# Up product of a conv-gated MLP: two groups of three tiles with two seven-product tiles each, and the first down sums behind tile 4

## The chip, the cores and the metric

One core of one Trainium2 chip. TensorE (PE) multiplies; VectorE (DVE) and ScalarE (ACT) work on vectors in SBUF and PSUM; GpSimd (POOL) works in SBUF; SyncE (SP) issues DMAs. Each engine takes its instructions in the order of its own queue, and engines wait for one another by semaphores. The metric is the device time of one execution in microseconds (us), the median of several runs.

## The reference

One layer of an encoder: a retention branch and a spatial-gating branch are merged and added to x, then comes a gated MLP with a depthwise convolution of width 3. Sequence 512, model width 1024, MLP width 2816, float32. The change touches only the MLP:

```python
def _conv_gated_mlp(h, w_up, conv_w, conv_b, w_down):
    hid = h @ w_up                      # (512, 1024) @ (1024, 5632)
    hid = lax.conv_general_dilated(hid, conv_w..., padding=((1, 1),), feature_group_count=c) + conv_b
    a, b = jnp.split(hid, 2, axis=-1)
    return (jax.nn.gelu(a) * b) @ w_down
```

Every float32 product is made of three matmuls in PE's float32r format, over a high part and a low part of each operand: high x high, high x low, low x high.

## The kernel before

The stages follow each other: projections with retention, the gates, the output product and norms, then the up product of the MLP and the down product.

**Up product.** The 5632 columns make 22 tiles (`NF`) of two blocks of 128 columns, one for each half of the gate. A block computed whole is 8 depth steps x 3 matmuls of 512 columns: `up_block`, through `mm3` (lines 231 to 233). Tiles 0 and 1 are early blocks, computed in two halves among the norms; tiles 2, 3, 20 and 21 are whole. Tiles 4 to 19 come in couples: the first of a couple as seven products, the second whole.

**Seven products.** A `Pair` treats the two blocks of a tile, the two halves of the depth and the two halves of the 512 positions as a 2 x 2 block product, and makes it in Winograd's way: seven products of 4 depth steps x 3 matmuls of 256 columns (line 691) in place of eight. The weights enter in seven forms: B11, B21, T1, T2, T3, T4, B22, where the T's are sums of raw weights; the activations' sums S1 to S4 were made once. `part1` does the products with B11, B21, T1 and T2; `part2` the one with T3 and takes T4 and B22; `part3` those two. A tile's three PSUM banks are summed into two temporaries c0 and c1 by ACT copies (line 85) and DVE sums (lines 708, 719, 731). The bank of the first product (B11) is written again by the fourth (T2), so that product must wait for the copy of c0 that reads the bank.

In a couple, PE's order is: `part1`; the first block of the whole tile; `part2`; half the second block; `part3`; the other half.

**Weights.** `units` lists what is loaded and in which order; `w_get` hands out the next and issues others ahead, as far as nine slots of the pool `w4` go (a form takes one slot, a block two). For each unit SP issues the load into one of four `raw` buffers; ACT copies it into the high part (wf, wh; line 85), DVE subtracts for the low part (wf, wl; line 92). For the T forms, DVE adds raw weights for T1 and T3 (lines 170, 171) and POOL for T2 and T4 (lines 172, 174): T2 = T1 + B22, T4 = T2 + B21, the latter written over T2's raw buffer once T2 is split.

**Behind a tile.** `tile_done` runs the convolution (`conv`: one ACT row and two DVE taps, lines 1000 and 1004, for each block), the GELU on ACT (line 1011) and the gate's product on DVE (line 1013). Then, after some tiles, `down_forms` makes the sums of the down product from two finished tiles: eight DVE rows (fa, fs, fl, gp; lines 92, 1030 to 1033) and four ACT copies. The first such sums, of tiles 0 and 1, stand behind tile 7.

The order in each engine's queue is set when the program is built; nothing is reordered on the chip between rows of DVE, ACT, POOL or SP.

Of the kernel before, what the change touches and what calls it, by code (L numbers as in the profile page):

```python
# [38 lines left out]
ENDS = (0, 2, 3, 1)  # L39
UP0 = DOWN0 - 2 * NF  # L40
EARLY = 4
COUPLES = [(i, i + 1) for i in range(4, 20, 2)]

PRE, LNG, LNB = 0, 8, 16
CW, CB = 24, 24 + 3 * 2 * NF
# [5 lines left out]
def tile_block(ctx: ExitStack, tc, xT, x, wall, par, cs, wsp, bsp, gpost, gpre, gffn, out):  # L51
# [11 lines left out]
    def blk(dt=F32, n="blk", shape=(P, S)):  # L63
        return sb.tile(list(shape), dt, tag="blk", bufs=NBLK, name=nm(n))
# [4 lines left out]
    def tmp(n="tmp", shape=(P, S)):  # L69
        return sb.tile(list(shape), F32, tag="tmp", bufs=6, name=nm(n))  # L70
# [7 lines left out]
    def ps(shape=(P, S)):  # L78
        return pp.tile(list(shape), F32, tag="ps", name=nm("ps"))
# [18 lines left out]
    FORMS = ("B11", "B21", "T1", "T2", "T3", "T4", "B22")  # L98
    units = []
    i = 0  # L100
    while i < NW:
        pair = [(f, i) for f in FORMS]
        if U0 <= i < GATE0:
            units += pair
            i += 2
        elif GATE0 <= i < GATE1:
            units += pair[:4] + [("blk", i + 2)] + pair[4:] + [("blk", i + 3)]
            i += 4
        elif i == UP0 + 2 * COUPLES[0][0]:
            for a, b in COUPLES:  # L110
                pair = [(f, UP0 + 2 * a) for f in FORMS]
                units += pair[:4] + [("blk", UP0 + 2 * b)] + pair[4:] + [("blk", UP0 + 2 * b + 1)]
            i = UP0 + 2 * COUPLES[-1][1] + 2
        elif i == DOWN0:
            for _ in range(2):
                pairs = [[("q", i + j), ("t", i + j)] for j in range(DP)]
                whole = [[("blk", i + DP)], [("blk", i + DP + 1)]]
                for u in pairs[:4] + whole[:1] + pairs[4:6] + whole[1:] + pairs[6:] if i == DOWN0 else pairs + whole:
                    units += u
                i += DP + WHOLE // 2  # L120
        else:
            units.append(("blk", i))
            i += 1
# [90 lines left out]
    def w_next():  # L214
        u = units[w_pos[1]]
        w_ready[w_pos[1]] = w_unit(u)
        w_pos[1] += 1
        return w_size(u)

    def w_get(look=LOOK, most=99):  # L220

        i = w_pos[0]
        w_pos[0] += 1
        room = 2 * look + (2 if w_size(units[i]) == 2 else 0)
        n = sum(w_size(u) for u in units[i : w_pos[1]])
        while w_pos[1] < len(units) and (w_pos[1] <= i or n + w_size(units[w_pos[1]]) <= min(most, max(room, 9 if look == LOOK else 0))):
            n += w_next()
        return w_ready.pop(i)

    def mm3(o, ah, al, bh, bl, start, stop):  # L230
        nc.tensor.matmul(o, ah, bh, start=start, stop=False)  # L231
        nc.tensor.matmul(o, ah, bl, start=False, stop=False)  # L232
        nc.tensor.matmul(o, al, bh, start=False, stop=stop)  # L233
# [48 lines left out]
    for k in range(KD):  # L282
# [18 lines left out]
        for m in range(8):  # L301
            c = slice(m * P, (m + 1) * P)
# [78 lines left out]
    for m in range(8):  # L381
        t = blk(n="qkraw")
# [266 lines left out]
    for n, acc in enumerate(t_group()):  # L649
        if n == 0:  # L650
            g_turn(0)
        if n < 2:
            for k in (n + 2, n + 6):
                t = tmp("xT")
# [92 lines left out]
    uT, late = [], None  # L747
    for j in range(KD // 2):
        p = Pair(AF.Gelu_apprx_tanh, lambda: blk(n="u"), scale=rbc)
# [7 lines left out]
        late = p  # L757
# [46 lines left out]
    for j in range(KD // 2):  # L804
        for o, t in gated_pair(ogh, ogl, late if j == 0 else None):
            b = blk(n="r")
# [117 lines left out]
    def h2(k, t):  # L924
        return tuple(h[k // 2][:, k % 2, t] for h in (h2h, h2l))

    h2forms = {n: [None] * 4 for n in ("S1", "S2", "S3", "S4")}
# [8 lines left out]
    def h2_sums(i):  # L936

        a0, b0, a1, b1 = h2r[0][i], h2r[0][i + 2], h2r[1][i], h2r[1][i + 2]
        v.tensor_sub(b1, a1, b1)
        v.tensor_sub(a1, a0, a1)  # L940
        v.tensor_sub(a0, b1, a0)
        v.tensor_add(b0, b0, a0)
        for n, t in zip(("S1", "S2", "S3", "S4"), (b1, a0, a1, b0)):
            h2_parts(n, i, t)
# [9 lines left out]
    def up_block(between=None):  # L954
        (wh, wl), o = w_get(), ps()
        for k in range(KD):
            if between and k == KD // 2:
                between()
            c = slice(k * P, (k + 1) * P)
            mm3(o, wh[:, c], wl[:, c], *h2(k, slice(0, S)), k == 0, k == KD - 1)  # L960
        return o
# [33 lines left out]
    def conv(o, m):  # L995
        c = tmp("cv")
        nc.scalar.activation(
            out=c, in_=o, func=AF.Identity, scale=col(CW + 3 * m + 1), bias=col(CB + m)
        )
        v.scalar_tensor_tensor(  # L1000
            out=c[:, 1:S], in0=o[:, 0 : S - 1], scalar=col(CW + 3 * m), in1=c[:, 1:S],
            op0=ALU.mult, op1=ALU.add,
        )
        v.scalar_tensor_tensor(
            out=c[:, 0 : S - 1], in0=o[:, 1:S], scalar=col(CW + 3 * m + 2), in1=c[:, 0 : S - 1],
            op0=ALU.mult, op1=ALU.add,
        )
        return c

    def gated(ca, cb):  # L1010
        nc.scalar.activation(out=ca, in_=ca, func=AF.Gelu_apprx_tanh)
        gp.append(blk(n="gp"))
        v.tensor_mul(gp[-1], ca, cb)
# [10 lines left out]
    def down_forms(j):  # L1024

        a, b = gp[2 * j], gp[2 * j + 1]
        first = blk(F32R, "fa")
        split(first[:, T0], first[:, T1], a[:, T0])
        s_ = blk(n="fs")
        v.tensor_sub(s_[:, T0], a[:, T1], b[:, T1])  # L1030
        v.tensor_sub(s_[:, T1], s_[:, T0], a[:, T0])
        v.tensor_sub(a[:, T0], a[:, T0], a[:, T1])
        v.tensor_add(a[:, T1], b[:, T0], s_[:, T1])
        bh, bl = two_parts(b, j >= WIDE)
        sh, sl = two_parts(s_, j >= WIDE)
        th, tl = two_parts(a, j >= WIDE)
        dforms.append({
            "A11": (first[:, T0], first[:, T1]), "A12": (bh[:, T0], bl[:, T0]), "A22": (bh[:, T1], bl[:, T1]),
            "S1": (sh[:, T0], sl[:, T0]), "S2": (sh[:, T1], sl[:, T1]),
            "S3": (th[:, T0], tl[:, T0]), "S4": (th[:, T1], tl[:, T1]),  # L1040
        })

    def tile_done(i, o):
        gated(*(conv(t, 2 * i + s_) for s_, t in enumerate(o)))
        if i < COUPLES[-1][1]:
            if i in (7, 11, 13, 17):
                down_forms(len(dforms))
        elif len(dforms) < EAGER:
            down_forms(len(dforms))

    couples = dict(COUPLES)
    i = 0
    while i < NF:
        if i in couples:
            p = Pair(None, lambda: tmp("c"), h2, h2forms)
            p.part1()
            o = [up_block()]
            p.part2()
            o.append(up_block(p.part3))
            tile_done(i, p.t)  # L1060
            tile_done(i + 1, o)
            i += 2
        else:
            o = []
            for e in (2 * i, 2 * i + 1):
                o.append(early_o[e] if e < EARLY else up_block())
            if i < 2:
                h2_sums(i)
                w_next()
            tile_done(i, o)  # L1070
            i += 1
# [154 lines left out]
    for t in ENDS:  # L1226
# [10 lines left out]
        for i, (b, e) in enumerate((((M2, e1), (M3, xx)), ((M4, uu), (M8, yy)))[t // 2]):  # L1237
            f, h = slice((t % 2) * 256, (t % 2 + 1) * 256), slice(i * 256, (i + 1) * 256)
# [51 lines left out]

def _up(a):

    for i, _ in COUPLES:
        b, c = a[2 * i].reshape(P, 2, S), a[2 * i + 1].reshape(P, 2, S)
        a[2 * i : 2 * i + 2] = np.stack([
            np.concatenate([b[:, 0], c[:, 0]], -1), np.concatenate([c[:, 1], b[:, 1]], -1),
        ])
    return a
# [85 lines left out]
```

## Time and profile before

| | |
|---|---|
| median of 3 runs | 818.98 us (818.52 to 819.2) |
| the profiled execution | 818.99 us |
| its span, first to last instruction | 817.2 us |
| mean granted clock of TensorE | 0.999 |
| busy: DVE, ACT, POOL | 657.0, 430.0, 102.5 us |
| instructions | 13212 |
| loads of raw weights on SP's queue | 145, 512 KB each, 3.5 us to landing |

The page of the profile has the busy time of each engine; its matmuls are pipelined, so that a busy PE alone says little, and the chain of work that ended last and the list of waits are read beside it. A timeline row has its start, its length, the engine, the line, the operation, what it writes and reads with buffer numbers left out, the shape, and in brackets the idle time before it. Rows overlap by some 0.1 us at their ends, so that the price of a row in a busy queue is the distance to the next start.

### The profile page before, as it was taken

The numbers are of one execution on the slowest core, as the hardware profiler recorded it, in microseconds if no ns is written. First come the engines' busy times: TensorE is split into PE (matmuls) and PEld (weight loads), VectorE is DVE, ScalarE is ACT, GpSimd is POOL, SyncE is SP. The second block draws the span as 40 slices with busy tenths as digits, with TensorE's granted clock in tenths as the row PEclk, the third lists the DMA queues.
The fourth block names the chain that finished last, engine by engine and source line by source line (L and its number), as shares of the span: only waits on it lengthen the run. The fifth ranks groups of instructions, "written<-read, shape, count | busy, mean of one in ns | idle before, by whom it ended". The sixth has DMA issues, their size and how long they took to land.

```text
span 817.2 us, 13212 instructions
## 1 busy us (share of the span) xinstructions
PE 810.2 (99%) x5154; PEld 730.9 (89%) x5154; DVE 657.0 (80%) x1076; ACT 430.0 (53%) x733; POOL 102.5 (13%) x108
## 2 busy tenths in 40 slices
PE   9999999999999999999999999999999999999997
PEld 7888888888899999999988898899999998999996
DVE  7579897877898877767766579778989989898976
ACT  6636445536665544444435466455656665645532
POOL 0100000012222011132211210210201200000001
PEclk9999999999999999999999999999999999999999
DMA  8733221222234332323359212333333341234354
GB/s 284 262 117 103 77 79 65 68 75 79 91 101 133 104 93 88 103 86 103 102 175 360 87 49 73 104 103 103 104 104 103 103 140 67 78 103 129 104 181 104
DMA packets 29391, 93.76 MB, mean 115 GB/s; under 512 B 3408, under 2 KB 4304, under 8 KB 29328
## 3 DMA queue, kind: packets, MB, share of 16 engines
q1 hardware_dynamic: 26928, 86.59, 32.1%
q0 software_dynamic: 1968, 6.03, 2.4%
q8 instruction: 40, 0.66, 0.4%
q10 hardware_dynamic: 432, 0.30, 0.1%
q14 instruction: 23, 0.19, 0.1%
HBM read 88.19 MB, written 4.72 MB: 114 GB/s over the span
## 4 chain that ended last, share of the span: by engine, by line
PE 98%; DMA 0%; DVE 0%; issue 0%; ACT 0%; DVEq 0%
PE ps L691 23%; PE ps L232 13%; PE ps L231 13%; PE ps L233 13%; PE ps L1088 11%; PE ps L495 5%; PE ps L496 5%; PE ps L497 5%; PE ps L1119 2%; PE ps L846 2%; PE ps L845 2%; PE ps L847 2%; PE ps L770 1%; PE ps L295 1%; PE ps L912 0%; PE ps L620 0%
## 5 line engine op out<-in xcount | busy, mean ns | idle before, releaser
L92 DVE TENSOR_TENSOR wl<-raw,wh 128x1024 fp32r<-128x1024 f32 (+1 forms) x93 | 108.9, 1180 | 48.2 <-PE ps L691 24.2
L85 ACT ACTIVATE wf<-raw 128x512 fp32r<-128x512 f32 x140 | 84.9, 626 | 98.7 <-PE ps L232 40.2
L92 DVE TENSOR_TENSOR wf<-raw,wf 128x512 fp32r<-128x512 f32 x140 | 110.0, 802 | 26.4 <-ACT wf L85 25.6
L691 PE MATMUL ps<-sh,wf 128*128 128x256 f32 x640 | 118.8, 277 | 0.0
L85 ACT ACTIVATE wh<-raw 128x1024 fp32r<-128x1024 f32 (+2 forms) x95 | 93.0, 989 | 34.5 <-DMA raw<-wall 16.5
L691 PEld LDWEIGHTS ps<-sh,wf 128*128 128x128 f32 x640 | 100.7, 188 | 0.9 <-ACT wf L85 0.2
L231 PE MATMUL ps<-h2h,wh 128*128 128x512 f32 (+1 forms) x256 | 93.2, 364 | 0.0
L232 PE MATMUL ps<-h2l,wh 128*128 128x512 f32 (+1 forms) x256 | 93.1, 364 | 0.0
L233 PE MATMUL ps<-h2h,wl 128*128 128x512 f32 (+1 forms) x256 | 92.8, 362 | 0.0
L691 PE MATMUL ps<-sl,wf 128*128 128x256 f32 x320 | 88.5, 277 | 0.0
L495 PE MATMUL ps<-wh,xh 128*128 128x512 f32 x192 | 75.1, 391 | 0.0
L496 PE MATMUL ps<-wl,xh 128*128 128x512 f32 x192 | 74.9, 390 | 0.0
L497 PE MATMUL ps<-wh,xl 128*128 128x512 f32 x192 | 74.8, 390 | 0.0
L172 POOL TENSOR_TENSOR raw<-raw,raw 128x512 f32<-128x512 f32 x20 | 33.9, 1693 | 239.5 <-DVE raw L170 185.9
L691 PEld LDWEIGHTS ps<-sl,wf 128*128 128x128 f32 x320 | 60.1, 188 | 0.8 <-issue 0.2
L233 PEld LDWEIGHTS ps<-h2h,wl 128*128 128x128 f32 x256 | 48.3, 189 | 7.7
L231 PEld LDWEIGHTS ps<-h2h,wh 128*128 128x128 f32 x256 | 48.2, 188 | 6.9
L232 PEld LDWEIGHTS ps<-h2l,wh 128*128 128x128 f32 x256 | 48.1, 188 | 6.5
L691 PE MATMUL ps<-xh,wf 128*128 128x256 f32 x288 | 53.4, 278 | 0.0
L1088 PE MATMUL ps<-dl,fh 128*128 128x256 f32 x168 | 46.5, 277 | 0.0
L1088 PE MATMUL ps<-dh,fl 128*128 128x256 f32 x168 | 46.5, 277 | 0.0
L1088 PE MATMUL ps<-dh,fh 128*128 128x256 f32 x168 | 46.5, 277 | 0.0
(326 smaller groups left out, 2057.9 us busy)
## 6 DMA issues: line engine op xcount, KB each, us to landing
raw<-wall SPq DMA_DIRECT2D x145, 512.0 KB, 3.5
x<-x SPq DMA_DIRECT2D x20, 256.0 KB, 5.5
xT<-xT SPq DMA_DIRECT2D x8, 256.0 KB, 5.5
x<-x POOLq DMA_DIRECT2D x8, 256.0 KB, 2.6
xT<-xT POOLq DMA_DIRECT2D x4, 256.0 KB, 3.9
cs<-cs SPq DMA_DIRECT2D x2, 256.0 KB, 4.2
gpm<-gpost POOLq DMA_DIRECT2D x2, 256.0 KB, 3.9
gpr<-gpre POOLq DMA_DIRECT2D x2, 256.0 KB, 5.0
```

What stands on the lines that cost most here:

```text
L85: nc.scalar.activation(out=o, in_=i, func=AF.Copy)
L92: return nc.vector.tensor_sub(lo, src, as32(hi))
L172: nc.gpsimd.tensor_tensor(out=w_raw["T2"], in0=w_raw["T1"], in1=w_raw["B22"], op=ALU.add)
L231: nc.tensor.matmul(o, ah, bh, start=start, stop=False)
L232: nc.tensor.matmul(o, ah, bl, start=False, stop=False)
L233: nc.tensor.matmul(o, al, bh, start=False, stop=stop)
L495: nc.tensor.matmul(acc[t], xh[k][:, c], wh[:, f], start=k == 0, stop=False)
L496: nc.tensor.matmul(acc[t], xh[k][:, c], wl[:, f], start=False, stop=False)
L497: nc.tensor.matmul(acc[t], xl[k][:, c], wh[:, f], start=False, stop=k == KD - 1)
L691: nc.tensor.matmul(o, w_[:, c], a_, start=first and k == n == 0, stop=k == 3 and n == 2, skip_group_check=True,)
L845: nc.tensor.matmul(o, ah, bh, start=k == 0, stop=False)
L1088: nc.tensor.matmul(o, a_[:, c], w_[:, f], start=j == t == i == 0, stop=j == DP - 1 and i == 2 and n not in (M2, M3, M4), skip_group_check= ...
```

## The change

Tiles 4 to 9 are no longer three couples but two groups of three, (4, 5, 6) and (7, 8, 9): in each the first two tiles are made as seven products, the third whole. Nine tiles instead of eight are made as seven products. In such a group, PE's order is: `part1` of the first tile; the first block of the whole tile; `part2` of the first tile; `part1` of the second; `part3` of the first; `part2` of the second; half the second block; `part3` of the second; the other half. The unit list follows: four forms, a block, ten forms, a block. `tile_done` of the first tile is called right after its `part3`. The first `down_forms` (tiles 0 and 1) moves from behind tile 7 to behind tile 4; those behind 11, 13 and 17 stay. On the host, the raw weights of each tile are laid out for the seven products or whole, as the new list wants. From tile 10 on the couples are as before.

```diff
-COUPLES = [(i, i + 1) for i in range(4, 20, 2)]
+GROUPS = [(4, 5, 6), (7, 8, 9)] + [(i, i + 1) for i in range(10, 20, 2)]
+SUMS_AT = (4, 11, 13, 17)
...
-        elif i == UP0 + 2 * COUPLES[0][0]:
-            for a, b in COUPLES:
-                pair = [(f, UP0 + 2 * a) for f in FORMS]
-                units += pair[:4] + [("blk", UP0 + 2 * b)] + pair[4:] + [("blk", UP0 + 2 * b + 1)]
-            i = UP0 + 2 * COUPLES[-1][1] + 2
+        elif i == UP0 + 2 * GROUPS[0][0]:
+            for *a, b in GROUPS:
+                group = [(f, UP0 + 2 * t) for t in a for f in FORMS]
+                units += group[:4] + [("blk", UP0 + 2 * b)] + group[4:] + [("blk", UP0 + 2 * b + 1)]
+            i = UP0 + 2 * GROUPS[-1][-1] + 2
...
-        if i < COUPLES[-1][1]:
-            if i in (7, 11, 13, 17):
+        if i < GROUPS[-1][-1]:
+            if i in SUMS_AT:
                 down_forms(len(dforms))
...
-    couples = dict(COUPLES)
+    groups = {g[0]: g for g in GROUPS}
...
-        if i in couples:
+        if i in groups:
             p = Pair(None, lambda: tmp("c"), h2, h2forms)
             p.part1()
             o = [up_block()]
             p.part2()
+            if len(groups[i]) > 2:
+                late, p = p, Pair(None, lambda: tmp("c"), h2, h2forms)
+                p.part1()
+                late.part3()
+                tile_done(i, late.t)
+                i += 1
+                p.part2()
             o.append(up_block(p.part3))
```

Lines below the edit in `tile_done` move down by one (a first product's sum stands at 709 instead of 708, a tap at 1001 instead of 1000). The places in the queues of which the prediction speaks:

ACT around the copy of tile 8's first product, before. c_991 is that copy; wf_975 and wf_996 are tile 8's T4 and B22, cv_980 and cv_981 rows of tile 7's convolution, wh_998 the second block of tile 9:

```order
L997 ACTIVATE cv_978_5728<-c_955_5537,part_63 128x512
L997 ACTIVATE cv_980_5735<-ps_969_5618,part_63 128x512
L1011 ACTIVATE cv_977_5724<-cv_977_5724 128x512
L85 ACTIVATE wf_975_5670<-raw_967_5611 128x512
L997 ACTIVATE cv_981_5739<-ps_976_5673,part_63 128x512
L85 ACTIVATE wf_996_5771<-raw_964_5589 128x512
L85 ACTIVATE c_991_5766<-ps_993_5768 128x256
L85 ACTIVATE wh_998_5802<-raw_997_5800 128x1024
```

The same copy in the change is c_997; wf_991, wf_992, wf_993, wf_995 and wf_996 are tile 8's T1, T2, T3, T4 and B22, c_981 belongs to tile 7, wh_1003 is the second block of tile 9:

```order
L86 ACTIVATE wf_991_5753<-raw_990_5749 128x512
L86 ACTIVATE wf_992_5769<-raw_990_5749 128x512
L86 ACTIVATE wf_993_5772<-raw_986_5714 128x512
L86 ACTIVATE c_981_5694<-ps_982_5695 128x256
L86 ACTIVATE wf_995_5801<-raw_990_5749 128x512
L86 ACTIVATE wf_996_5818<-raw_987_5715 128x512
L86 ACTIVATE wh_1003_5828<-raw_1002_5826 128x1024
L86 ACTIVATE c_997_5821<-ps_999_5823 128x256
```

Tile 8's T1 to T4 now come directly ahead of the copy, and the block, formerly behind it, ahead of it too. In between, before, stood rows of a whole tile's convolution.

DVE around the first down sums (fa, fs, fl and gp_885 rows), in the change. gp_958 is tile 4's gated product, c_943 belongs to tile 5, wl_970 is the first block of tile 9, wf_971 tile 7's T3, and wf_955 (ahead of all this) tile 7's T1:

```order
L1014 TENSOR_TENSOR gp_958_5568<-cv_956_5559,cv_957_5563 128x512
L93 TENSOR_TENSOR fa_959_5570<-gp_885_5126,fa_959_5570 128x256
L1031 TENSOR_TENSOR fs_960_5573<-gp_885_5126,gp_899_5163 128x256
L1032 TENSOR_TENSOR fs_960_5573<-fs_960_5573,gp_885_5126 128x256
L93 TENSOR_TENSOR fl_962_5579<-gp_899_5163,fh_961_5578 128x512
L1033 TENSOR_TENSOR gp_885_5126<-gp_885_5126 128x256
L93 TENSOR_TENSOR fl_964_5583<-fs_960_5573,fh_963_5582 128x512
L1034 TENSOR_TENSOR gp_885_5126<-gp_899_5163,fs_960_5573 128x256
L93 TENSOR_TENSOR wl_970_5610<-raw_968_5607,wh_969_5609 128x1024
L93 TENSOR_TENSOR wf_971_5613<-raw_950_5478,wf_971_5613 128x512
L93 TENSOR_TENSOR fl_966_5587<-gp_885_5126,fh_965_5586 128x512
L732 TENSOR_TENSOR c_943_5455<-ps_946_5458,c_943_5455 128x256
```

Before, the same sums stood behind tile 7's convolution, among the forms of tiles 8 and 10. Further down the same queue, where tile 8's forms begin (cv_977, cv_978: tile 6's convolution; wf_985: tile 7's B22; wf_988, wf_989, wf_991, wf_992: tile 8's B11, B21, T1, T2; raw_990 the raw sum for T1):

```order
L1001 SCALAR_TENSOR_TENSOR cv_978_5686<-ps_973_5620,part_63,cv_978_5686 128x511
L93 TENSOR_TENSOR wf_985_5698<-raw_951_5479,wf_985_5698 128x512
L1005 SCALAR_TENSOR_TENSOR cv_978_5686<-ps_973_5620,part_63,cv_978_5686 128x511
L93 TENSOR_TENSOR wf_988_5718<-raw_986_5714,wf_988_5718 128x512
L1014 TENSOR_TENSOR gp_979_5691<-cv_977_5682,cv_978_5686 128x512
L709 TENSOR_TENSOR c_980_5693<-ps_983_5696,c_980_5693 128x256
L93 TENSOR_TENSOR wf_989_5734<-raw_987_5715,wf_989_5734 128x512
L171 TENSOR_TENSOR raw_990_5749<-raw_986_5714 128x512
L172 TENSOR_TENSOR raw_986_5714<-raw_986_5714,raw_987_5715 128x512
L93 TENSOR_TENSOR wf_991_5753<-raw_990_5749,wf_991_5753 128x512
L93 TENSOR_TENSOR wf_992_5769<-raw_990_5749,wf_992_5769 128x512
L93 TENSOR_TENSOR wf_993_5772<-raw_986_5714,wf_993_5772 128x512
```

Two tiles' and a whole tile's convolutions and the down sums stand in one stretch of the queue ahead of tile 8's raw sums: 34 rows from tile 4's last c (`c_926`) to raw_990.

More of the change, by code (lines that the diff above doesn't have):

```diff
@@ L1291, in _up @@
 def _up(a):
-    for i, _ in COUPLES:
+    for i in (t for g in GROUPS for t in g[:-1]):
         b, c = a[2 * i].reshape(P, 2, S), a[2 * i + 1].reshape(P, 2, S)
```

## The prediction, made before the change was run

> **What bounds the kernel now.** I read the page first: the busy shares, then the chain that ended last, then the list of waits of TensorE (PE).
>
> ```profile
> PE 810.2 (99%) x5154; PEld 730.9 (89%) x5154; DVE 657.0 (80%) x1076; ACT 430.0 (53%) x733; POOL 102.5 (13%) x108
> PE 98%; DMA 0%; DVE 0%; issue 0%; ACT 0%; DVEq 0%
> PE ps L280 <- DVE raw L275: 1.0, 1, 1.0
> ```
>
> PE's matmuls are the chain (98%), and its only wait in the whole run is 1.0 us before the warm-up. So the time is the sum of PE's matmuls. An edit can gain only by taking matmul time away, and it loses by every us in which it makes PE wait. Next, the up stage by couples of tiles, from the first product of tiles 4, 6 and 8 on, and below them a stretch of an earlier stage that is seven-product work alone (columns: stretch, its length, busy time and count of PE, PEld, DVE, ACT, POOL, then granted clock, DMA share, GB/s):
>
> ```profile
> 517.02:537.52 20.50, 20.50 (x133) 18.57 (x132) 13.90 (x20) 10.49 (x19) 2.93 (x2) 1.00 0.28 96
> 537.52:558.02 20.50, 20.50 (x133) 18.57 (x132) 15.70 (x25) 11.20 (x20) 2.94 (x2) 1.00 0.32 103
> 558.02:578.52 20.50, 20.50 (x133) 18.57 (x132) 19.85 (x32) 12.70 (x23) 2.94 (x2) 1.00 0.28 88
> 226.00:246.00 20.00, 20.00 (x179) 20.00 (x178) 19.78 (x31) 13.61 (x25) 4.57 (x4) 1.00 0.33 106
> ```
>
> Each couple takes 20.50 us at full clock. VectorE (DVE) has room in the first two and almost none in the third (19.85 of 20.50), the one with down sums in it. DVE is the second limit, and the change loads it.
>
> **The gain on PE.** Two cuts of PE's timeline give the prices: the ends of a block and of four products.
>
> ```profile
> 506.14 0.39 PE L231 MATMUL ps<-h2h,wh 128*128 128x512 f32 x1
> 511.58 0.39 PE L231 MATMUL ps<-h2h,wh 128*128 128x512 f32 x1
> 537.52 0.28 PE L691 MATMUL ps<-h2h,wf 128*128 128x256 f32 x1
> 542.97 0.40 PE L231 MATMUL ps<-h2h,wh 128*128 128x512 f32 x1
> ```
>
> A whole block is 24 matmuls of 512 columns: 511.58 - 506.14 = 5.44 us, 226.7 ns each. Four products are 48 matmuls of 256 columns: 542.97 - 537.52 = 5.45 us, 1.363 us a product, 113.5 ns a matmul, exactly half. A couple is therefore 7 x 1.363 = 9.54 for the seven products and 20.50 - 9.54 = 10.96 for the two blocks between them. A group of three is 14 x 1.363 + 10.96 = 30.04. Two groups take 60.08 us where three couples took 61.50: **-1.42 us**, and that is all that can be gained. The five later couples and everything behind them keep their matmuls.
>
> The page "TensorE: Matmul & The Clock Gate" of the Trainium skill, "Back-to-back issue gap", speaks against this edit: it gives sustained spacings of 81 ns for 128 columns and 131 ns for 512, so far from proportional. As an estimate from that page, a straight line between them puts 256 columns at 98 ns, 84 x 98 = 8.2 us against 48 x 131 = 6.3 us for a tile, and each converted tile would lose. The rows above disagree with it, 113.5 against 226.7 ns, and the measurement decides.
>
> **The price on DVE.** The order of the engines' rows is fixed in the program, so the cost is read from queues. DVE's prices stand in the stretch of the before that holds the down sums (a row's price is its start to the next start):
>
> ```profile
> 562.85 0.75 DVE L1004 SCALAR_TENSOR_TENSOR cv<-ps,part,cv 128x511 f32<-128x511 f32 x1
> 563.51 0.42 DVE L708 TENSOR_TENSOR c<-ps,c 128x256 f32<-128x256 f32 x1
> 563.84 0.68 DVE L1013 TENSOR_TENSOR gp<-cv,cv 128x512 f32<-128x512 f32 x1
> 564.44 0.42 DVE L92 TENSOR_TENSOR fa<-gp,fa 128x256 fp32r<-128x256 f32 x1
> 564.78 0.42 DVE L1030 TENSOR_TENSOR fs<-gp,gp 128x256 f32<-128x256 f32 x1
> 565.11 1.22 DVE L92 TENSOR_TENSOR wl<-raw,wh 128x1024 fp32r<-128x1024 f32 x1
> 566.25 0.42 DVE L1031 TENSOR_TENSOR fs<-fs,gp 128x256 f32<-128x256 f32 x1
> ...
> 568.45 1.30 DVE L92 TENSOR_TENSOR wf<-raw,wf 128x512 fp32r<-128x512 f32 x2
> 569.66 0.69 DVE L92 TENSOR_TENSOR fl<-gp,fh 128x512 fp32r<-128x512 f32 x1
> 570.26 0.69 DVE L170 TENSOR_TENSOR raw<-raw 128x512 f32<-128x512 f32 x1
> 570.99 0.69 DVE L171 TENSOR_TENSOR raw<-raw,raw 128x512 f32<-128x512 f32 x1
> ```
>
> So: a tap of the convolution (cv) 0.66, a 256-wide sum (c) 0.33, a 512-wide row (wf, gp, fl) 0.60, a block's low part (wl) 1.14, and the eight rows of down sums 564.44 to 565.11, 566.25 to 568.45 and 569.66 to 570.26, together 3.47 us.
>
> A converted tile adds seven wf, two sums of raw weights and three c and drops two wl: 7 x 0.60 + 1.3 + 1.0 - 2.3 = 4.2 us of DVE for 1.34 us less of PE. By itself that fits: the first couples leave 6.6 and 4.8 us of DVE idle. But the down sums, formerly behind tile 7, now stand behind tile 4, in the middle of the first group. What is late is what waits behind them in the queues, and the order shows one thing that PE waits for: the copy by ScalarE (ACT) of a tile's first product, c0. PE's fourth product (T2) accumulates into the bank that this copy reads.
>
> When is tile 8's copy due? Tile 7 starts at 517.02 + 30.04 = 547.06, and tile 8's product with T2 comes four products, a block (5.48), one product and three more products later: 547.06 + 5.45 + 5.48 + 1.36 + 4.09 = **563.44**.
>
> When does it end? In ACT's queue it stands directly behind the copies of tile 8's T4 and B22 forms and of a whole block. T4 comes from a POOL sum, that from DVE's split of T2, that from a first POOL sum, that from DVE's sum of raw weights for T1.
> - DVE's start: its row for tile 4's last c waits for B22 of tile 4, which PE ends 4 + 1 + 4 + 2 products and a block behind 517.02, at 537.5. The seven rows ahead of it start when PE has done B21 of tile 5, whose slot the first of them writes (532.0, and 0.25 for the wait) and cost 1.14 + 0.33 + 5 x 0.6 to 0.7, to 536.9, plus one POOL sum that holds DVE up (below). I take 537.7.
> - From that c to tile 8's raw sum, the order counts 34 rows: 12 cv (7.92), 6 wf (3.60), 3 gp (1.80), 4 c (1.32), 1 wl (1.14), the 8 down sums (3.47): 19.25 us. With 0.5 for short waits (the third couple above has 0.65 idle in all) the raw sum starts at 537.7 + 19.25 + 0.5 = 557.45.
> - The chain from there, as it ran for tile 10, where the raw sum started at 570.26:
>
> ```profile
> 571.18 1.64 POOL L172 TENSOR_TENSOR raw<-raw,raw 128x512 f32<-128x512 f32 x1 [19.45 <-DVE raw L170]
> 574.29 1.30 POOL L174 TENSOR_TENSOR raw<-raw,raw 128x512 f32<-128x512 f32 x1 [1.47 <-DVE wf L92]
> 524.35 1.78 DVE L92 TENSOR_TENSOR wf<-raw,wf 128x512 fp32r<-128x512 f32 x1
> 559.59 0.62 ACT L85 ACTIVATE wf<-raw 128x512 fp32r<-128x512 f32 x1
> 560.12 0.37 ACT L85 ACTIVATE c<-ps 128x256 f32<-128x256 f32 x1
> 560.38 1.06 ACT L85 ACTIVATE wh<-raw 128x1024 fp32r<-128x1024 f32 x1
> 561.34 0.62 ACT L1011 ACTIVATE cv<-cv 128x512 f32<-128x512 f32 x1
> 643.51 0.37 ACT L85 ACTIVATE c<-ps 128x256 f32<-128x256 f32 x1
> ```
>
> 570.26 to 574.29 + 1.30 is 5.33 us. POOL's sum takes 1.64 instead of 1.30 when a DVE row is under way, and now T3's split stands right behind T2's: 0.34 more. So the T4 sum ends at 557.45 + 5.67 = 563.12. Then ACT: two wf (0.53 each, 559.59 to 560.12), the block (0.96, 560.38 to 561.34), the copy (0.37): 2.39. It ends at 565.51, **2.07 us late**. In the before the same copies were in time: tile 8's at 560.12 + 0.37, due at 558.02 + 4.09 = 562.11, and the tightest, tile 16's, ended at 643.88, 0.23 ahead of 640.02 + 4.09 (tile 16 starts four couples of 20.50 behind 558.02).
>
> Tile 7's copy is late too, but inside this: it stands behind a GELU that needs 23 of the rows, 12.65 us with the down sums, so it ends near 537.7 + 12.65 + 0.5 + 0.52 + 0.37 = 551.7 where 547.06 + 4.09 = 551.15 is due. That 0.6 delays PE, not DVE's chain, and so is part of the 2.07. Without the down sums there, tile 8's copy would end at 562.0, in time: **moving them costs the whole stall**, and takes 3.47 us from DVE in a later stretch, where PE never waited, which is worth nothing.
>
> At nothing I also cost: the block's low part in the middle of a group (ready near 533.5, used at 517.02 + 20.46 + 1.36 = 538.8), the 36 more weight loads (they lie inside the spacing above), SP's queue (the same transfers in the same order), PSUM (3 + 3 + 2 = 8 banks; tile 8 reuses those of tile 6, whose last tap stands five rows, 2.1 us, ahead of the raw sum, so at 555.3, for use at 547.06 + 12.29 = 559.35).
>
> Bounds of the stall: none, if DVE reaches the raw sum 2.07 us earlier; and each of the two POOL sums on the way can hold a DVE row for 1.78 - 0.69 = 1.1 us, of which 0.34 is counted, so up to 2.07 + 1.9 = 4.0 us. I take 2.07, because the rows it is made of are all priced back to back. **Sum:** -1.42 + 2.07 = +0.65 us. The profiled execution took 818.99 us (span 817.2 and 1.8 around it), the median of the runs is 818.98, so the sum carries over: 819.6 us.
>
> **Rivals.** (1) No stall or a small one (below 1.2 us): DVE gets there earlier, since part of the rows may run while PE's products are still outstanding. Against it stand 19.25 us of rows in one queue. 818.99 - 1.42 = 817.6, up to 818.8. (2) **Slower:** the same copy, later. The mechanism is DVE held by POOL's sums in a queue with no idle time; it decides when tile 8's raw sum starts behind 558.4, 1 us later than I work out: then the stall passes 3.1 us and the time 820.6, to 821.5 at the upper bound. For it: one such hold costs up to 1.1 us. Against: I have counted a usual share. (3) The change makes runs of eight products (10.9 us) where the up stage had four, and weight loads may then set a wider spacing. From 10.88 / 84 = 129.5 ns on a converted tile loses; at 150 ns in the 16 products of the two runs, 192 x 36.5 ns = 7.0 us, the time would be 824.6 without any stall. Against it stands the stretch 226 to 246: PEld is busy all 20.00 us and 179 matmuls touch it, some two of them only at its edge, so 113 ns in a run far longer than eight. The page of the skill named above takes this rival's side.
>
> **How the numbers follow.** The forecast, a stall of 1.2 to 3.0 us (818.8 to 820.6): 0.60. Rival 1 (817.6 to 818.8): 0.17. Rival 2 (820.6 to 821.5): 0.22. Rival 3: 0.01. 0.2% is 1.64 us, about what a measurement here can tell from no change: faster needs less than 817.34, which even the whole gain misses by 0.24; the runs of the before spread over 0.7 us, so I give it 0.03. Slower is rivals 2 and 3, 0.23; within, 0.74. The range takes in the bounds of the stall up to where a tenth is left on each side: 817.5 to 821.2.
>
> **What would show it.** 60.1 us and the stall between tiles 4 and 10; two waits of PE for ACT's c, the first near 551 below 1 us and the second near 563.4 of 1 to 2 us, none elsewhere; tile 8's raw sum on DVE near 557.5; DVE without idle time from 541 to 557. The prediction is wrong if PE waits for a form or a bank instead, if a copy in the second group is in time, or if the products' spacing in the groups isn't 113.5 ns.

## The result, and the profile after

| | before | changed |
|---|---|---|
| median, 6 runs each | 818.79 us (818.35 to 819.2) | 821.65 us (821.45 to 822.08) |
| ratio, 95% interval | | 1.0035 [1.0025, 1.0045] |
| profiled execution, its span | 818.99 us, 817.2 | 821.45 us, 819.3 |
| time around the span | 1.78 us | 2.10 us |

The change makes the kernel slower by 2.86 us, 0.45 us past the upper end of the range. The page of the changed kernel, in the order in which the page of before was read: busy times, the chain that ended last by engine, and TensorE's (PE's) waits.

```profile
PE 810.5 (99%) x5190; PEld 732.0 (89%) x5190; DVE 665.3 (81%) x1086; ACT 434.0 (53%) x742; POOL 107.2 (13%) x110
PE 95%; DMA 2%; DVE 1%; ACT 1%; issue 0%; DVEq 0%; POOLq 0%; POOL 0%; ACTq 0%
PE ps L692 <- ACT c L86: 2.1, 1, 2.1
PE ps L281 <- DVE raw L276: 1.0, 1, 1.0
```

The chain no longer is PE alone, and one wait is new: a seven-product matmul waits for a copy by ScalarE (ACT), once, for 2.1 us. Busy shares hardly moved; they would not have told. The stretches of the changed kernel, cut at the first products of tiles 4, 7, 10 and 12, and then two short ones behind the new wait (columns as in the prediction: stretch, length, busy time and count of PE, PEld, DVE, ACT, POOL, then granted clock, DMA share, GB/s):

```profile
516.75:546.76 30.01, 30.01 (x217) 28.08 (x216) 25.18 (x38) 17.68 (x33) 6.47 (x4) 1.00 0.26 80
546.76:580.80 34.04, 31.98 (x218) 29.41 (x216) 32.15 (x48) 20.27 (x36) 6.88 (x4) 0.95 0.31 97
580.80:601.30 20.50, 20.50 (x134) 18.56 (x132) 17.03 (x26) 12.17 (x22) 2.94 (x2) 1.00 0.36 122
554.52:557.94 3.42, 3.42 (x12) 2.84 (x11) 3.42 (x7) 0.90 (x2) 0.00 (x0) 0.50 0.21 50
557.94:563.04 5.10, 5.10 (x29) 4.42 (x29) 4.92 (x7) 1.79 (x3) 2.07 (x2) 1.00 0.17 69
```

The first group takes 30.01 us, as worked out, and the next couple 20.50. The second group takes 34.04, 4.0 more than the first. Its granted clock is 0.95 in the mean; the fourth row shows why: for 3.42 us it is 0.50, and then 1.00 again. The page's clock line of 40 slices prints 9 everywhere, because a slice is 20 us long. PE's rows at that place:

```profile
550.85 0.40 PE L232 MATMUL ps<-h2h,wh 128*128 128x512 f32 x1
553.31 0.39 PE L692 MATMUL ps<-sh,wf 128*128 128x256 f32 x1 [2.06 <-ACT c L86]
555.10 0.63 PE L233 MATMUL ps<-h2l,wh 128*128 128x512 f32 x1
555.52 0.63 PE L234 MATMUL ps<-h2h,wl 128*128 128x512 f32 x1
```

The row at 550.85 is a matmul of tile 9's first block that runs ahead of the product that waits. The row behind it was due 0.227 later, at 551.08. It is tile 7's product with T2, and it starts at 553.31: 2.23 us lost. From 554.5 on, 512 columns take 0.42 instead of 0.227: 1.7 us lost over 3.42. So the second group's excess of 4.0 us is a wait and a slow clock, 3.9 together. ACT's queue ahead of the copy that PE waited for:

```profile
549.59 0.81 ACT L998 ACTIVATE cv<-c,part 128x512 f32<-128x512 f32 x1 [1.00 <-DVE c L732]
550.31 1.43 ACT L998 ACTIVATE cv<-ps,part 128x512 f32<-128x512 f32 x2
551.84 0.63 ACT L86 ACTIVATE wf<-raw 128x512 fp32r<-128x512 f32 x1
552.38 0.61 ACT L1012 ACTIVATE cv<-cv 128x512 f32<-128x512 f32 x1
552.90 0.36 ACT L86 ACTIVATE c<-ps 128x256 f32<-128x256 f32 x1
```

The last row is tile 7's copy. It ends at 553.26, and nothing in it waits for PE: ACT idles 1.00 us for a sum on VectorE (DVE), then runs convolution, a form, the GELU and the copy back to back. DVE's queue up to that sum and beyond, down to tile 8's raw sum (L171), and behind it GpSimd's (POOL's) T2 and T4 sums of tile 7 and of tile 8:

```profile
535.11 0.69 DVE L172 TENSOR_TENSOR raw<-raw,raw 128x512 f32<-128x512 f32 x1 [0.35 <-DMA raw<-wall]
535.79 2.32 DVE L93 TENSOR_TENSOR wf<-raw,wf 128x512 fp32r<-128x512 f32 x2
538.03 0.41 DVE L732 TENSOR_TENSOR c<-ps,c 128x256 f32<-128x256 f32 x1
539.63 0.74 DVE L1005 SCALAR_TENSOR_TENSOR cv<-c,part,cv 128x511 f32<-128x511 f32 x1
540.29 1.79 DVE L1001 SCALAR_TENSOR_TENSOR cv<-c,part,cv 128x511 f32<-128x511 f32 x1
542.00 0.41 DVE L720 TENSOR_TENSOR c<-ps,c 128x256 f32<-128x256 f32 x1
...
549.13 0.42 DVE L732 TENSOR_TENSOR c<-ps,c 128x256 f32<-128x256 f32 x1
551.39 1.41 DVE L1005 SCALAR_TENSOR_TENSOR cv<-c,part,cv 128x511 f32<-128x511 f32 x2
558.68 0.69 DVE L171 TENSOR_TENSOR raw<-raw 128x512 f32<-128x512 f32 x1
```

```profile
535.26 1.69 POOL L173 TENSOR_TENSOR raw<-raw,raw 128x512 f32<-128x512 f32 x1 [7.74 <-DMA raw<-wall]
539.78 1.74 POOL L175 TENSOR_TENSOR raw<-raw,raw 128x512 f32<-128x512 f32 x1 [2.83 <-DVE wf L93]
559.50 1.74 POOL L173 TENSOR_TENSOR raw<-raw,raw 128x512 f32<-128x512 f32 x1 [17.98 <-DVE raw L171]
562.71 1.67 POOL L175 TENSOR_TENSOR raw<-raw,raw 128x512 f32<-128x512 f32 x1 [1.47 <-DVE wf L93]
```

Twice DVE rows run long while a POOL sum of tile 7 is under way: the two wf rows from 535.79 take 2.24 to the next start where two cost 1.2 elsewhere (POOL's T2 sum runs to 536.95), and the convolution row at 540.29 takes 1.79 where its neighbour takes 0.74 (POOL's T4 sum runs to 541.52). Each hold (a DVE row made longer while POOL's sum runs) costs DVE about 1.05 us, and the rows behind them leave next to no idle time to make it up. Ahead of the first hold DVE also waits 0.35 us for a load of raw weights, at 535.11. Tile 8's copy, the one that the prediction was built on:

```profile
564.42 1.16 ACT L86 ACTIVATE wf<-raw 128x512 fp32r<-128x512 f32 x2 [0.79 <-POOL raw L175]
565.48 1.04 ACT L86 ACTIVATE wh<-raw 128x1024 fp32r<-128x1024 f32 x1
566.43 0.36 ACT L86 ACTIVATE c<-ps 128x256 f32<-128x256 f32 x1
```

It ends at 566.79. In a group without any loss PE would have needed it at 563.17 (the prediction's 563.44, less 0.27 because tile 4 began at 516.75 and not 517.02): 3.6 us late. PE came 3.9 us late itself, and so shows no wait here.

### The profile page after: what moved, and what is told of

It is laid out like the page before. It is cut to its first block, busy times and chain, and to the rows that moved or that the text cites. A ratio compares the mean times of both kernels' runs of the same rounds, so it can differ in the third digit from the quotient of the medians.

```text
span 819.3 us, 13316 instructions
## 1 busy us (share of the span) xinstructions
PE 810.5 (99%) x5190; PEld 732.0 (89%) x5190; DVE 665.3 (81%) x1086; ACT 434.0 (53%) x742; POOL 107.2 (13%) x110
## 4 chain that ended last, share of the span: by engine, by line
PE 95%; DMA 2%; DVE 1%; ACT 1%; issue 0%; DVEq 0%; POOLq 0%; POOL 0%; ACTq 0%
PE ps L692 23%; PE ps L233 12%; PE ps L232 12%; PE ps L234 12%; PE ps L1096 10%; PE ps L496 5%; PE ps L497 5%; PE ps L498 5%; PE ps L1127 2%; PE ps L848 2%; PE ps L847 2%; PE ps L846 2%; DMA raw<-wall 1%; PE ps L771 1%; PE ps L296 1%
## 5 line engine op out<-in xcount | busy, mean ns | idle before, releaser
L86 ACT ACTIVATE wf<-raw 128x512 fp32r<-128x512 f32 x147 | 89.6, 626 | 101.2 <-PE ps L233 37.9
L93 DVE TENSOR_TENSOR wl<-raw,wh 128x1024 fp32r<-128x1024 f32 (+1 forms) x91 | 105.9, 1173 | 44.5 <-PE ps L692 17.1
L93 DVE TENSOR_TENSOR wf<-raw,wf 128x512 fp32r<-128x512 f32 x147 | 116.1, 806 | 25.8 <-ACT wf L86 24.7
L692 PE MATMUL ps<-sh,wf 128*128 128x256 f32 x672 | 125.1, 278 | 2.1 <-ACT c L86 2.1
L692 PEld LDWEIGHTS ps<-sh,wf 128*128 128x128 f32 x672 | 105.9, 188 | 3.2 <-ACT c L86 2.4
L692 PE MATMUL ps<-sl,wf 128*128 128x256 f32 x336 | 93.0, 277 | 0.0
L232 PE MATMUL ps<-h2h,wh 128*128 128x512 f32 (+1 forms) x240 | 87.4, 364 | 0.0
L233 PE MATMUL ps<-h2l,wh 128*128 128x512 f32 (+1 forms) x240 | 87.3, 364 | 0.0
L234 PE MATMUL ps<-h2h,wl 128*128 128x512 f32 (+1 forms) x240 | 86.9, 362 | 0.0
L692 PEld LDWEIGHTS ps<-sl,wf 128*128 128x128 f32 x336 | 63.2, 188 | 0.8 <-issue 0.2
```

Of the source, the lines that this page charges most:

```text
L86: nc.scalar.activation(out=o, in_=i, func=AF.Copy)
L93: return nc.vector.tensor_sub(lo, src, as32(hi))
L692: nc.tensor.matmul(o, w_[:, c], a_, start=first and k == n == 0, stop=k == 3 and n == 2, skip_group_check=True,)
```

## The experiments

The first reading (A in the expectations): the loss lies in DVE's and ACT's queues ahead of the first products' copies, loaded by the groups, the down sums and POOL's sums together; the half clock costs nothing of its own, because tile 8's copy would have stopped PE at the same point. Against it stand: the down sums alone cost it (B); the half clock is a loss on top (C); and, for the later runs, that groups of three load the engines too much wherever the sums stand (D), and that the remedies bring something by themselves (E). The kernels were timed in three batches, each on one chip and beside the kernel before, which took 818.66 to 818.79 us in them. The order of the rows in the queues is built anew for each kernel, so that an edit also moves rows that it doesn't name (with T4's sums on DVE, a block's low part comes to stand among the down sums).

**Down sums moved, couples kept.**

```diff
 # the kernel before
-            if i in (7, 11, 13, 17):
+            if i in (4, 11, 13, 17):
```

> The couples of before, with the first down sums behind tile 4 in place of 7: the second half of the change alone. Theory A (DVE is late in the groups, ACT's copy of a first product is late behind it, PE waits): in couples DVE has 4.8 to 6.6 us idle at that place, so no wait of PE and the time of before, 818.5 to 819.2. Theory B (moving the sums costs by itself): a wait of PE near tile 6's or 8's copy and 820.5 or more.

818.7 us against 818.79, ratio 0.9999 [0.999, 1.0008], and no new wait between the tiles. With couples, the eight DVE rows behind tile 4 cost nothing.

**Groups kept, down sums back behind tile 7.**

```diff
-SUMS_AT = (4, 11, 13, 17)
+SUMS_AT = (7, 11, 13, 17)
```

> The two groups of three, with the first down sums behind tile 7 as before: the first half of the change alone. Theory A: the 3.5 us of sums no longer stand ahead of tile 7's and tile 8's copies, so the wait of 2.1 us at 551 to 553 is gone and tile 8's copy waits below 1 us; the sums now fall behind the second group, where a wait may come at tile 10's copy. 817.4 to 820.2. If the grouping alone makes the wait, it stays at tile 7's copy with about 2 us and the time is 821 to 822.

820.37 us, ratio 1.0022 [1.0013, 1.0032]: still slower than before. The wait at tile 7's copy is gone; another stands at tile 10's. PE's rows there, with the idle time in brackets:

```profile
582.14 0.39 PE L234 MATMUL ps<-h2h,wl 128*128 128x512 f32 x1
584.41 0.38 PE L692 MATMUL ps<-sh,wf 128*128 128x256 f32 x1 [1.88 <-ACT c L86]
```

Between these two places, the place of the sums decides which copy is late, not whether one is. B falls: the sums are free among couples, and the groups lose with the sums left where they were.

**PE kept busy through the wait.** 32 matmuls of 256 columns, into a part of a bank that a later product starts anew: 20 ahead of tile 7's product with T2 and 12 ahead of tile 8's.

```diff
-        def part1(self):
+        def part1(self, fill=0):
...
+            h_ = self.act(0, T0)[0]
+            for _ in range(fill):
+                nc.tensor.matmul(self.b[2][:, T1], h_[:, :P], h_, start=False, stop=False, ...)
```

> The change, with matmuls that compute nothing used in the two places where PE would wait: 20 of 256 columns (2.3 us) ahead of tile 7's product with T2, 12 (1.4 us) ahead of tile 8's. They write the unused half of a bank. PE stays busy, so the granted clock should stay at 1.0. Theory A (the half clock is masked, since tile 8's copy is 3.6 us late whatever PE does): 821.0 to 821.6, within 0.6 of the change. Theory C (the half clock adds its 1.7 us): 819.7 to 820.2.

821.65 us, ratio 1.0035 [1.0022, 1.0047], the same as the changed kernel. The granted clock is 1.00 throughout and PE waits nowhere there. The two rows that matter, on PE and on ACT:

```profile
551.17 2.56 PE L713 MATMUL ps<-h2h 128*128 128x256 f32 x20
```

```profile
566.62 0.37 ACT L86 ACTIVATE c<-ps 128x256 f32<-128x256 f32 x1
```

Tile 8's copy ends at 566.99, 49.93 us behind that kernel's first product of tile 4 (517.06); in the changed kernel it is 566.79 - 516.75 = 50.04. So with a full clock DVE's chain is no earlier, and PE would have been stopped at the same point. C, which needed a gain, falls. The fillers hold PE 2.4 us at tile 7 (the product behind them starts at 553.57, 6.49 behind tile 7's first, where 4.09 is due); tile 8's copy is due 5.45 + 5.48 + 1.36 + 4.09 = 16.38 us behind tile 7's first product at 547.08, and with those 2.4 at 565.86, so PE would wait 1.1 us more: 3.5 of the 3.9 us are lost at any clock, and the half clock is worth 0.4 at most. The six runs of the changed kernel agree: four with a mean clock of 0.996 or 0.997 took 821.45 to 822.08 us, two with 0.999 took 821.68 and 821.77.

**T4's sum on DVE in the groups, down sums left behind tile 4.**

```diff
+T4_ON_DVE = range(8, 20)
...
-            nc.gpsimd.tensor_tensor(out=w_raw["T4"], ...)
+            engine = nc.vector if i - UP0 in T4_ON_DVE else nc.gpsimd
+            engine.tensor_tensor(out=w_raw["T4"], ...)
```

> The change, with the raw sum for T4 of tiles 4, 5, 7 and 8 made on DVE (0.6 us more in its queue each) and not on POOL. Theory A with POOL's hold: the convolution row that took 1.79 us at 540.3 takes 0.75 again, tile 7's copy comes 0.5 to 1 us earlier, the wait there is 1.0 to 1.7 us, and the chain ahead of tile 8's copy loses a POOL sum and two hand-overs; 819.5 to 821.2. If ACT's own queue or the loads set the copy: the wait stays at 2.1 us and 821.4 or more.

820.92 us (820.06 to 824.46), ratio 1.003 [1.0019, 1.0041]. The loss at tile 7's copy falls from 2.23 to 1.16 us, but only 0.36 of it because the copy is earlier (it ends at 553.07, 36.15 us behind tile 4's first product at 516.92; in the change 36.51): the hold of 1.05 us is gone, and the T4 sum itself stands in DVE's queue for 0.60. The rest is order: four matmuls of tile 9's block run ahead of the waiting product, where in the change one did. And two new waits stand further on, for a copy and for a sum on DVE, both ahead of tile 8's last two products:

```profile
574.03 0.39 PE L694 MATMUL ps<-h2h,wf 128*128 128x256 f32 x1 [1.07 <-ACT c L87]
576.87 0.39 PE L694 MATMUL ps<-sh,wf 128*128 128x256 f32 x1 [1.14 <-DVE c L722]
```

What PE doesn't lose at tile 7 it loses one tile later. DVE's queue shows what stands ahead of these two:

```profile
569.54 0.69 DVE L173 TENSOR_TENSOR raw<-raw,raw 128x512 f32<-128x512 f32 x1 [1.25 <-DMA raw<-wall]
574.71 1.77 DVE L1003 SCALAR_TENSOR_TENSOR cv<-c,part,cv 128x511 f32<-128x511 f32 x1
```

A load of raw weights is waited for 1.25 us, the two wf rows behind it are held by POOL's T2 sum of tile 10, from 569.69 (2.26 us instead of 1.2), and the convolution row is held by POOL's T4 sum of tile 10, from 574.20, which this edit leaves on POOL. Why the load comes late was not followed up.

**Both: first down sums behind tile 11, and T4's sums on DVE for tiles 4 to 19.**

```diff
-SUMS_AT = (4, 11, 13, 17)
+T4_ON_DVE = range(8, 40)
+SUMS_AT = (11, 13, 15, 17)
```

> The changed kernel with the down sums behind tiles 11, 13, 15 and 17 and the T4 sum of every tile from 4 to 19 on VectorE. Theory A (the whole loss is the wait for the first product's copy and the half clock behind it; the queue of VectorE and ScalarE ahead of that copy was made late by the down sums and by GpSimd's T4 sum, which also holds VectorE): with both away no wait for the copies of tiles 7, 8 and 10 is left, the clock stays full, and the spacing gain of 1.42 us shows alone: 817.2 to 817.8, faster than both kernels, ratio 0.998 to 0.999. Theory D (the groups of three load VectorE and ScalarE past what they can do between tiles 4 and 10, wherever the sums stand): a wait of 1 to 2 us moves to a later copy (tile 10's or 12's, or one of a block), 818.5 to 820.5.

817.21 us (816.85 to 817.67) against 818.7, ratio 0.9982 [0.9973, 0.999]: faster than both kernels. Stretches from tile 4's first product to tile 10's, and on to the last matmul:

```profile
517.23:577.27 60.04, 60.04 (x433) 56.17 (x432) 55.02 (x83) 37.19 (x66) 6.70 (x4) 1.00 0.32 105
577.27:809.56 232.29, 232.29 (x1706) 218.65 (x1705) 210.96 (x350) 129.34 (x213) 11.24 (x11) 1.00 0.33 110
```

60.04 us for the two groups, without a wait and at full clock. DVE is busy 55.02 of them, so it is not overloaded in the mean (D falls). Its rows at the place of the second hold, where L177 is tile 7's T4 sum:

```profile
539.67 0.74 DVE L1007 SCALAR_TENSOR_TENSOR cv<-c,part,cv 128x511 f32<-128x511 f32 x1
540.34 0.74 DVE L1003 SCALAR_TENSOR_TENSOR cv<-c,part,cv 128x511 f32<-128x511 f32 x1
541.00 0.41 DVE L722 TENSOR_TENSOR c<-ps,c 128x256 f32<-128x256 f32 x1
541.33 0.73 DVE L1007 SCALAR_TENSOR_TENSOR cv<-c,part,cv 128x511 f32<-128x511 f32 x1
541.99 0.68 DVE L177 TENSOR_TENSOR raw<-raw,raw 128x512 f32<-128x512 f32 x1
```

The row that took 1.79 takes 0.74 again, and the sum itself costs DVE 0.60: doing POOL's work took DVE less time than standing still beside it, by 0.45 us. Moving the T4 sums does a second thing: tile 8's own T4 sum stands in the chain ahead of tile 8's copy. From its raw sum to the end of T4's sum that chain takes 4.67 us here (554.88 to 559.55), where it took 5.70 in the change. So the shorter chain brings more for tile 8's copy than the hold that is gone.

**The same two edits with couples**, as a control.

> The kernel before (eight couples) with the same two edits: down sums behind tiles 11, 13, 15 and 17, the T4 sum of tiles 4 to 18 on VectorE. It is the control of the kernel with groups of three that has both edits. There is no wait of TensorE between tiles 4 and 20 to remove in the kernel before, so theory A expects no change, 818.6 to 819.0; the difference from the groups is then the spacing gain alone, 1.4 us. Theory E (the two edits bring a gain of their own, or a wait of their own): 817.5 to 818.3, or 819.5 and more.

818.94 us (818.2 to 819.21, and one run of 821.14 of which no trace was kept), ratio 1.0003 [0.9994, 1.0012]. They bring nothing by themselves (E falls). The two kernels differ by 818.94 - 817.21 = 1.7 us, for a difference of 61.50 - 60.04 = 1.46 in the stretch.

**Down sums behind tile 11, T4's sums left on POOL** (the list of places alone).

> The changed kernel with the down sums behind tiles 11, 13, 15 and 17 alone; the T4 sum stays on GpSimd. It tells the place of the sums from GpSimd's hold. If the sums in the run between tiles 4 and 12 are the larger cause (VectorE's 34 rows and the queue behind them), what is left is one short wait, below 1 us, at the copy of tile 8, with a full clock: 817.8 to 818.8. If GpSimd's sum and its hold of VectorE's rows are enough for a loss by themselves, a wait of 1 us or more stands at tile 7's, 8's or 10's copy: 818.8 to 820.5.

819.0 us, ratio 1.0002 [0.9993, 1.001]: no different from the kernel before. Most of the loss is gone, but not all. Two waits of PE for a copy are left, at tile 8's and far behind the groups; then, from DVE's queue, the convolution row that POOL's T4 sum holds, as in the changed kernel:

```profile
563.99 0.38 PE L692 MATMUL ps<-sh,wf 128*128 128x256 f32 x1 [0.31 <-ACT c L86]
664.54 0.39 PE L692 MATMUL ps<-sh,wf 128*128 128x256 f32 x1 [0.36 <-ACT c L86]
```

```profile
540.69 1.78 DVE L1001 SCALAR_TENSOR_TENSOR cv<-c,part,cv 128x511 f32<-128x511 f32 x1
```

The starts of PE's two rows lie 0.48 and 0.52 us behind their due times. The two stretches lose 1.10 and 0.70 us in all (table below); the rest are delays of 0.1 to 0.3 us between PE's rows, which the list of waits doesn't have. The expectation of one wait and 818.8 at most was somewhat low.

**Down sums behind tile 9, T4's sums on DVE.**

> The changed kernel with the down sums behind tiles 9, 11, 13 and 17 and the T4 sum of tiles 4 to 19 on VectorE. The sums behind tile 9 stand in front of what tile 10 needs: with the sums behind tile 7, tile 10's copy was waited for 1.9 us, with GpSimd's T4 sum in place. If the sums' place decides, a wait for tile 10's copy of 0.5 to 2 us is left: 818 to 819.5. If the T4 sum on GpSimd was the larger part there, no wait is left: 817.2 to 817.8, as with the sums behind tile 11.

817.23 us, ratio 0.9981 [0.9972, 0.999], 60.04 and 232.29 us in the two stretches, no wait: as good as behind tile 11.

**The same with T4's sum on DVE for tile 8 alone** (`T4_ON_DVE = (16, 17)`).

> The changed kernel with the down sums behind tiles 9, 11, 13 and 17 and the T4 sum on VectorE for tile 8 alone (the other eight tiles' T4 sums stay on GpSimd, so that GpSimd runs 108 instructions, as in the kernel before). Two questions. First, how much of the T4 edit the groups need: if tile 8's copy was the only late one left, 817.2 to 817.8, as with all nine on VectorE; if GpSimd's sums also make the later copies late (tile 10's behind the sums of tile 9, or one near 664), a wait of 0.5 to 2 us, 818 to 819.5. Second, the time around the span: it is 1.78 us in the kernel before and in every kernel with at most 108 GpSimd instructions so far, 2.10 in those with 110. If the number of GpSimd's instructions decides, 1.78 here; if the groups with GpSimd's sums do, 2.10.

819.56 us, ratio 1.0011 [1.0002, 1.002]. PE's waits, in total, with their number and the longest:

```profile
PE ps L694 <- ACT c L87: 0.7, 2, 0.4
PE ps L694 <- DVE c L722: 0.6, 1, 0.6
PE ps L298 <- DVE wh L154: 0.2, 1, 0.2
```

The one for DVE stands at 573.50, the two for copies behind the groups, at 623.50 and 644.69. None stands at tile 8's copy. So it isn't tile 8's copy alone: with the other tiles' T4 sums back on POOL, waits are left that the kernel above doesn't have. (POOL runs 109 instructions here, not the 108 of the expectation; the time around the span is 1.82 us.)

**Two more POOL sums, with couples.** Tile 18's T2 sum is made three times with the same values.

```diff
 # the kernel before
             nc.gpsimd.tensor_tensor(out=w_raw["T2"], ...)
+            if i - UP0 in (36, 37):
+                nc.gpsimd.tensor_tensor(out=w_raw["T2"], ...)
+                nc.gpsimd.tensor_tensor(out=w_raw["T2"], ...)
```

> The kernel before (eight couples) with two more GpSimd instructions: tile 18's T2 sum is made three times over, the same values each time, so that GpSimd runs 110 instructions, as in the changed kernel. If their number decides the time around the span, it is 2.10 us here (1.78 before); if the groups of three do, 1.78. The copy of tile 18 stands 3.5 us later by GpSimd's time (two sums of 1.74 us), so a wait of TensorE near the last couple of 0 to 3.5 us may come with it: 818.7 to 822.5; the span tells it from the time around.

820.77 us, ratio 1.0025 [1.0015, 1.0036]. The two added sums on POOL, and what PE then waits for:

```profile
652.87 1.62 POOL L174 TENSOR_TENSOR raw<-raw,raw 128x512 f32<-128x512 f32 x1
654.57 1.27 POOL L175 TENSOR_TENSOR raw<-raw,raw 128x512 f32<-128x512 f32 x1
```

```profile
656.82 0.39 PE L694 MATMUL ps<-h2h,wf 128*128 128x256 f32 x1 [1.56 <-ACT c L85]
```

The time around the span is 1.85 us, not 2.10, so the number of POOL's instructions doesn't explain that term. The run does show how little slack such a copy has: two sums of 1.62 and 1.27 us ahead of it on POOL cost PE 234.24 - 232.29 = 1.95 us.

All kernels in one table, from the windows of their profiled runs: the stretch from tile 4's first product to tile 10's, from there to the last matmul, the mean time around the span, and the median of all runs (a profiled run lies up to 0.5 us from it, the one with "4, DVE in the groups" at 821.44).

| first down sums, T4's sum | tiles 4 to 10 | to the last matmul | around | median |
|---|---|---|---|---|
| couples: 7, POOL (before) | 61.50 | 232.29 | 1.78 | 818.79 |
| couples: 4, POOL | 61.50 | 232.29 | 1.78 | 818.70 |
| couples: 11, DVE | 61.50 | 232.29 | 1.78 | 818.94 |
| couples: 7, POOL with two sums more | 61.50 | 234.24 | 1.85 | 820.77 |
| groups: 4, POOL (the change) | 64.05 | 232.29 | 2.10 | 821.65 |
| groups: 7, POOL | 60.52 | 234.46 | 2.12 | 820.37 |
| groups: 4, POOL, PE filled | 64.02 | 232.29 | 2.09 | 821.65 |
| groups: 4, DVE in the groups | 64.23 | 232.29 | 1.77 | 820.92 |
| groups: 11, POOL | 61.14 | 232.99 | 2.12 | 819.00 |
| groups: 9, DVE for tile 8 | 60.95 | 233.76 | 1.82 | 819.56 |
| groups: 11, DVE | 60.04 | 232.29 | 1.77 | 817.21 |
| groups: 9, DVE | 60.04 | 232.29 | 1.78 | 817.23 |

The account closes: for the change, 64.05 - 61.50 = 2.55, and 2.10 - 1.78 = 0.32 around the span, 2.87 in all against 2.86 between the medians. For the best kernels -1.46 stands against -1.49 and -1.47.

## Why the prediction was wrong, point by point

- **The gain on PE: right.** 30.04 us were worked out for a group and 30.01 were measured in the first; the two groups take 60.04 without a stall, where 60.08 was forecast. -1.46 instead of -1.42. The wider spacing of the third rival didn't come.
- **The stall of 2.07 us: the term that was mis-sized.** It is 64.05 - 60.04 = 4.0 us, at the very end of the bounds given for it, and its mechanism (a first product's copy, late through ACT's queue, which is late through DVE's) is the one that was forecast. Tile 8's copy was 3.6 us late, 1.55 more than forecast. Step by step, in the frame of a tile 4 that starts 0.27 earlier: tile 4's last c on DVE began at 538.03 instead of 537.43 (+0.60); the 34 rows and their waits took 20.65 instead of 19.75 (+0.90); from the raw sum to the end of T4's sum 5.70 instead of 5.67, and ACT's part 2.41 instead of 2.39. The chain behind the raw sum was right, and so were the prices of undisturbed rows. What was wrong is **POOL's hold of DVE**: the start counted 0.8 for tile 7's T2 sum, which took 1.04; tile 7's T4 sum falls among the 34 rows and took 1.05 there, against 0.5 that was set aside for all short waits. The prediction had the price of such a hold, 1.1, but used it as a bound for the two sums behind tile 8's raw sum, and never asked which POOL sums run beside the 34 rows. The rest of the +0.60 is the wait of 0.35 us for a load of raw weights at 535.11: loads and SP's queue had been put at nothing. The whole miss is 2.86 - 0.65 = 2.2 us: 1.55 by this copy, some 0.4 by the half clock (below) and 0.3 around the span.
- **Tile 7's copy, "0.6 late and inside the 2.07": wrong in size, right in nature.** It was forecast to end at 551.7 (551.4 in this frame) and ended at 553.26. +0.60 is the late start again, +0.95 the 23 rows to the GELU's input (14.10 instead of 13.15: the hold of 1.05 is in it), and +0.25 that ACT began the GELU behind a form's copy and not at once. That PE's delay there doesn't delay DVE's chain is borne out: with fillers PE was 2.4 us late behind tile 7 and not 3.9, and tile 8's copy came at the same time.
- **Where PE waits: half right.** Two waits were forecast, the larger second. There was one, at tile 7; the half clock behind it then carried PE past the second in the profiled run.
- **The clock: a term that was absent.** No step had a clock below full. It cost 1.7 us in its stretch and at most 0.4 of the total.
- **"Moving them costs the whole stall": wrong.** With the sums behind tile 7 the loss is 2.04 us at tile 10's copy; with the sums behind tile 11 there still is 0.48 at tile 8's copy, which was to be in time at 562.0 and ends at 563.93 there. Both remedies were needed for the loss to vanish: the four kernels with places 4 and 11 and T4's sums on POOL and DVE took 821.65, 820.92, 819.0 and 817.21 us (the second with DVE for the groups' sums alone).
- **The time around the span: taken as 1.8 and was 2.10.** That is 0.3 us of the miss, and no run explains it.
- **The second rival was what happened.** Its point was a raw sum of tile 8 behind 558.4; it began at 558.68. Its mechanism was POOL's hold of DVE, its time 820.6 to 821.5; measured 821.65, of which 0.3 lie around the span. What it didn't have is that PE waited at tile 7's copy and not at tile 8's. It had a chance of 0.22, and the forecast 0.60, on the argument that a usual share of the hold was counted.

## What to carry to other kernels

An engine that is busy four fifths of its time has no slack in a stretch where its rows stand back to back: walk the queue row by row, and where a row of a second engine holds it up, count the whole hold. Moving a small sum onto the engine that it would hold can be cheaper than leaving it where it seems free, and it can shorten a chain that went over to the second engine and back. When a wait goes, look for the next one in the same queue: here the copies of tiles 7, 8, 10 and later ones were late in turn, and the matmul time saved showed only when all were in time.

## What the runs showed of the hardware that was not expected

- One wait of PE of 2.06 us was followed, 1.2 us after it ended, by 3.42 us at a granted clock of 0.50, then 1.00 again. Waits of 1.88 us (sums behind tile 7) and of 1.07 and 1.14 us (T4's sums on DVE) left the clock full in their profiled runs; so did one of 1.56 us (two more POOL sums). The fillers removed the wait and the half clock together: without them four of six runs had a mean clock of 0.996 or 0.997, with them all five had 0.998 or 0.999. That speaks for PE's idle time as the cause; where the limit lies isn't shown, nor why two runs of the change kept 0.999. The Trainium skill, page "TensorE: Matmul & The Clock Gate", part "The HAM clock gate", gives half clock after an idle window of about 3.4 us; the 3.42 us at half clock agree with such a window, but here 2.06 us without a matmul were enough. The run of 824.46 us among those with T4's sums on DVE had a mean clock of 0.995, and two of 821.4 and 822.24 us with the sums behind tile 7 had 0.996: their longer times speak for a loss that nothing hid, but no trace of them was kept.
- A POOL sum of two SBUF operands held a DVE row of the convolution with operands in SBUF too: 1.79 us instead of 0.74, beside a POOL sum of 1.74 us (1.30 in a row of the before). Such a sum on DVE took 0.68. The Trainium skill, page "SBUF — State Buffer", part "Who interferes with whom", states that a VectorE instruction with two inputs in SBUF contends with a GpSimd instruction that reads SBUF, through a port pair which is locked by one of them at a time. These rows agree with it in kind.
- The time around the span is 2.09 to 2.12 us in the four kernels with groups and all T4 sums on POOL, and 1.77 to 1.85 in all others. Neither the groups nor the number of POOL's instructions alone does it; what does stays open.
